# Attention scores by pairs of heads: cross products over 128 rows, high-by-high products over 64 rows each, in the two halves of the array

## The chip, the cores and the metric

The kernel runs on one core of one Trainium2 chip. A core has TensorE (PE; the profile lists its weight loads apart, as PEld), VectorE (DVE), ScalarE (ACT), GpSimd (POOL) and the queues that issue DMAs, SyncE's (SP) among them. The metric is the time of one execution on the device in microseconds, a median over runs. A difference below 0.2% of it, some 3.4 us, is about what a measurement of this kernel can't tell from no change.

## The reference

Two layers of a diffusion backbone with 512 latent tokens and 256 context tokens, width 1024. The change is in the first layer's attention: 16 heads of 64 channels, four key heads, queries in blocks of 128 tokens. A latent block reads all context keys and the latent keys of its own and its neighbouring blocks.

```python
def block(b):
    ...
    s_ctx = jnp.einsum('bqkgd,bnkd->bkgqn', qb, k_c, preferred_element_type=jnp.float32) * scale
    s_loc = jnp.einsum('bqkgd,bnkd->bkgqn', qb, kb, preferred_element_type=jnp.float32) * scale
    s_loc = jnp.where(valid, s_loc, NEG_INF)
    sink_col = jnp.broadcast_to(sink_g, s_ctx.shape[:-1] + (1,))
    p = jax.nn.softmax(jnp.concatenate([s_ctx, s_loc, sink_col], axis=-1), axis=-1).astype(vb.dtype)
    return (jnp.einsum('bkgqn,bnkd->bqkgd', p[..., :L], v_c)
            + jnp.einsum('bkgqn,bnkd->bqkgd', p[..., L:L + band], vb))
...
q_c = rms_norm((h_c @ w_qkv[:, :qd]).reshape(B, L, N_HEADS, HEAD_DIM), q_gain)
...
s_c = jnp.einsum('bqkgd,bnkd->bkgqn', q_c, k_c, preferred_element_type=jnp.float32) * scale
```

After the attention come its output projection, a SwiGLU feed-forward layer, the second layer's retention and another feed-forward layer. None of these is touched.

## The kernel before

Matrix products are made exact enough by splitting each fp32 operand into a high part, rounded to the array's reduced format (fp32r), and a low part, the remainder. A product of two split operands is then the sum of high by high, high by low and low by high; the projections (`mm3`, L147 to L149) spend one matmul on each of the three.

For the scores a head has only 64 channels, and the kernel uses the array's 128 rows for both parts at once. `make_q` leaves a tile for each head: for an even head `qa` has the high part in rows 0 to 63 and the low part in rows 64 to 127, for an odd head `qb` has them the other way round or, where the tiles are filled by DMA (pairs of heads 2 to 6, L605), the same way round as `qa`. `key_parts` leaves two tiles for each key head: `k1` with high over low, `k2` with low over high. A score is the query tile times `k1` plus the query tile times `k2` (L710): the four products high by high, low by low, high by low and low by high in two matmuls of 128 rows, which accumulate in one PSUM bank.

`attend(g, s, b)` works through one block of 128 queries of the four heads that share key head `g`, for stream `s` (0 latent, 1 context). There are 24 such blocks: for each key head four latent ones and two context ones. `Block.score(i)` makes the scores of head `i`. By the keys that a block reads there are three kinds: the first and last latent blocks have 256 latent and 256 context keys in one bank of 512 columns (two parts), the middle ones 256 context and 384 latent keys in two banks, one after the other (two runs), context blocks 256 keys in one bank. After each bank VectorE adds the mask, takes the minimum and writes the scores out of PSUM (L711). After each second head the softmax follows for the two: L717, the exponentials on ScalarE (L101), L721, the scaling (L725 on ScalarE, L727 on VectorE). Then `turn` transposes the probabilities on TensorE (L736) and copies them out (L738), and `output` multiplies them by the values (L750), which writes the two pairs of heads side by side into 64 partitions each.

The score banks come from a pool of three (`pS`, tile S), so that the fourth bank in the order of the program has to wait until L711 has read the first.

The order within an engine is set by a scheduler, ahead of time: in this stage only the dependences are given, and it interleaves the scores, transposes and value products with the projections of the next heads' queries (L147 to L149). What stands in the order waits for what is ahead of it on the same engine.

Of the kernel before, what the change touches and what calls it, by code (L numbers as in the profile page):

```python
# [8 lines left out]
F32 = mybir.dt.float32  # L9
# [3 lines left out]
ALU = mybir.AluOpType  # L13

P = 128
# [29 lines left out]
PRB = 9  # L45
# [4 lines left out]
def dit_kernel(ctx, tc, xT, cT, crow, small, consts, masks, tabs0, tabs1, jtab, adaQ, adaN, adaT, wst, out):  # L50
    nc = tc.nc
    mult, add, sub = ALU.mult, ALU.add, ALU.subtract
# [9 lines left out]
    def T(pool, cols, tag, bufs, dt=F32):  # L62
        return pool.tile([P, cols], dt, tag=tag, bufs=bufs, name=tag)

    def pj(n=512):
        return T(psJ, 512, "pj", 2)[:, :n]
# [24 lines left out]
    def after(ins, others):  # L91
        for o in others:
            tc.add_manual_dep(ins.ins, o.ins.name, order, reason="table set turn")
# [42 lines left out]
    def next_w(pool, own=2, raw=None, behind=(), late=()):  # L136

        raw = raw or w_raw()
        w = w_parts(pool, own)
        after(split(raw, *w, behind), late)  # L140
        return w
# [259 lines left out]
    mask = T(akv, NM * P, "mask", 1, BF16)  # L401
# [118 lines left out]
    ap = At.enter_context(tc.tile_pool(name="ap", bufs=1, reuse_waits="tile"))  # L520
# [3 lines left out]
    kx, kc = {}, {}  # L524
# [32 lines left out]
    q, stats = {}, {}  # L557

    def make_q(j, raw=None):

        if raw is None:
            w = next_w(ap, 0)
            parts_of = lambda k: (w[0][:, k * P:(k + 1) * P], w[1][:, k * P:(k + 1) * P])
        else:

            rows = [[T(ap, 656, "pr", PRB, F32R)[:, :512] for _ in range(2)] for _ in range(2)]
            for i, (hi, lo) in enumerate(rows):
                split(raw[:, i * 512:(i + 1) * 512], hi, lo)  # L570
            parts_of = lambda k: [t[:, k % 4 * P:(k % 4 + 1) * P] for t in rows[k // 4]]
        qs = T(ap, 64, "qs", 4)[:, 0:36].rearrange("p (f n) -> p f n", f=3)
        sqs, o = [], [None, None]

        def part(s, k0, k1):
            if k0 == 0:
                o[s] = pj(NTOK[s])
            for k in range(k0, k1):
                mm3(o[s], parts_of(k), h[s][k], k == 0, k == KT - 1)

        def shape(s):
            n = NTOK[s]
            sq, qn = t_sq(n), t_hn(n)
            nc.scalar.activation(qn, o[s], AF.Identity, scale=qk_gain[:, 0:1])
            nc.scalar.activation(sq, o[s], AF.Square)
            sqs.append(sq)
            if s == 0:
                sw = t_y(s)
                nc.vector.stream_shuffle(sw, qn, swap16)
                nc.vector.tensor_tensor(qn, qn, rope0[:, 0:512], op=mult)  # L590
                nc.vector.tensor_tensor(sw, sw, rope0[:, 512:1024], op=mult)
                nc.vector.tensor_tensor(qn, qn, sw, op=add)
            qa = T(ap, 512, "q", 9, F32R)
            if s == 0:
                qb = T(ap, 512, "q", 9, F32R)
            else:
                qa, qb = qa[:, 0:SC], qa[:, SC:2 * SC]
            q[2 * j, s] = qa
            q[2 * j + 1, s] = qb
            if 1 < j < 7:  # L600
                hi, lo = T(rp, 512, "y0", 1, F32R)[:, :n], T(rp, 512, "hn", 2, F32R)[:, :n]
                split(qn, hi, lo)
                for e, t in enumerate((qa, qb)):
                    for half, src in enumerate((hi, lo)):
                        nc.sync.dma_start(t[64 * half:64 * half + 64, :].bitcast(F32), src[64 * e:64 * e + 64, :].bitcast(F32))  # L605
                return
            nc.scalar.copy(qa[0:64, :], qn[0:64, :])
            nc.scalar.copy(qb[64:128, :], qn[64:128, :])
            nc.vector.tensor_tensor(qa[64:128, :], qn[0:64, :], qa[0:64, :], op=sub)
            nc.vector.tensor_tensor(qb[0:64, :], qn[64:128, :], qb[64:128, :], op=sub)  # L610

        def norms():
            tot = pj(12)
            for s, sq in enumerate(sqs):
                for b in range(NTOK[s] // P):
                    c = 8 * s + 2 * b
                    nc.tensor.matmul(tot[:, c:c + 2], sq[:, b * P:(b + 1) * P], bd[:, 0:P:64], start=True, stop=True)
            y, u, z = qs[:, 0], qs[:, 1], qs[:, 2]
            neg_half_rstd(y, z, tot, HD)
            nc.vector.scalar_tensor_tensor(u, tot, HD * EPS, y, add, mult)  # L620
            ue = u.rearrange("p (b e) -> p e b", e=2)
            for e in range(2):
                hd = 2 * j + e
                nc.vector.tensor_scalar(ue[:, e], ue[:, e], nsink[:, hd:hd + 1], -4.0 / HD, op0=mult, op1=mult)
                stats[hd] = qs

        def first():
            part(0, 0, 5)

        def second():  # L630
            part(0, 5, KT)
            shape(0)
            part(1, 0, 3)

        def third():
            part(1, 3, KT)
            shape(1)

        return [first, second, third, norms]
# [29 lines left out]
    pS = lambda: T(psA2, 512, "S2", 3)  # L669
# [5 lines left out]
    class Block:  # L675
# [9 lines left out]
        def score(self, i):  # L685
            g, s, b, n = self.g, self.s, self.b, len(self.keys) * P
            hd, nl = 4 * g + i, len(self.lk) * P
            if i % 2 == 0:
                self.st = T(ap, 16, "stat", 4)
            st, c = self.st, 2 * (b + 4 * s)  # L690
            qt = q[hd, s][:, b * P:(b + 1) * P]
            pt = T(ap, 656, "pr", PRB)[:, :n + 1]
            top = stats[hd][:, 1, c + hd % 2:c + hd % 2 + 1]
            nc.gpsimd.tensor_copy(pt[:, n:n + 1], top)
            lo, x0 = st[:, i % 2:i % 2 + 1], self.lk[0] * P if nl else 0

            if nl == 384:
                runs = [(nl, SC, 5 * P, [(0, SC, kc)]), (0, nl, 2 * P, [(0, nl, kx)])]
            elif nl == 0:
                runs = [(0, SC, 5 * P, [(0, SC, kc)])]  # L700
            elif b == 0:
                runs = [(0, n, 3 * P, [(0, nl, kx), (nl, SC, kc)])]
            else:
                runs = [(0, n, 0, [(0, SC, kc), (SC, nl, kx)])]
            for c0, w, m0, parts in runs:
                bank = pS()[:, :w]
                for p0, pw, kk in parts:
                    for r in range(2):
                        keys = kk[g][r] if kk is kc else kk[g][r][:, x0:x0 + pw]
                        nc.tensor.matmul(bank[:, p0:p0 + pw], qt, keys, start=r == 0, stop=r == 1)  # L710
                nc.vector.tensor_tensor_reduce(pt[:, c0:c0 + w], bank, mask[:, m0:m0 + w], 1.0, top, add, ALU.min, lo)  # L711
                top = lo
            self.pr.append(pt)
            if i % 2 == 0:
                return
            y = stats[hd][:, 0, c:c + 2]
            nc.vector.scalar_tensor_tensor(st[:, 2:4], st[:, 0:2], -1.0, y, mult, mult)  # L717
            for e in range(2):
                pt = self.pr[i - 1 + e]
                lnexp(pt, pt, AF.Exp, scale=y[:, e:e + 1], bias=st[:, 2 + e:3 + e], accum_out=st[:, 4 + e:5 + e])  # L720
            nc.vector.reciprocal(st[:, 6:8], st[:, 4:6])  # L721
            for e in range(2):
                pt = self.pr[i - 1 + e]
                if e:
                    nc.scalar.activation(pt[:, :n], pt[:, :n], AF.Identity, scale=st[:, 6 + e:7 + e])  # L725
                else:
                    nc.vector.tensor_scalar(pt[:, :n], pt[:, :n], st[:, 6 + e:7 + e], None, op0=mult)  # L727
            if i == 3:
                self.tt = []

        def turn(self, ki):
            if ki >= len(self.keys):
# [33 lines left out]

    def attend(g, s, b):
        blk = Block(g, s, b)
        for i in range(4):
            blk.score(i)  # L770
        for ki in range(len(blk.keys)):
            blk.turn(ki)
        blk.output()
        return blk.copy
# [94 lines left out]
    for d4 in range(0, KT, 4):  # L869
        wpos[0] = wo0 + max(d4, 2)  # L870
        w = [next_w(wo_p) if d > 1 else wo_w[d] for d in range(d4, d4 + 4)]
# [45 lines left out]
    bank = lambda n: T(psF, 512, n, 2)[:, 0:384]  # L917
# [448 lines left out]
    for hd in range(RH):  # L1366
# [24 lines left out]
        Y, X, kc = W4("Y"), W4("X"), W4("X")  # L1391
        kt, qt = [[T(qa, 512, "gate", 4) for _ in range(2)] for _ in range(2)]
# [144 lines left out]
        for i in range(2):  # L1537
            g, v = chunk(bg + i), chunk(bv + i)
# [16 lines left out]
        r, z = mv[:, 8:12], mv[:, 12:16]  # L1555
# [56 lines left out]
        w = []  # L1612
# [190 lines left out]
    for gsz in FFN_GROUPS:  # L1803
        acts = []
        for i in range(gsz):
            if f < 2:
                acts.append(first[f])
            elif f == 2:
                w = [next_w(fp, behind=norm_end) for _ in range(2)]
# [154 lines left out]
```

## Time and profile before

| | us |
|---|---|
| median of 3 runs (lowest to highest) | 1724.65 (1722.21 to 1725.27) |
| the profiled execution, its own time | 1725.47 |
| its span in the profile | 1723.7 |
| attention stage, from the first score to the last | 99 to 304 |

The profiled execution is 0.8 us above the median and 1.8 us longer than its span. In the profile a line names the place in the kernel: L710 is the score product, L711 the reduction behind it, L736 the transposes, L750 the value products. A matmul's row has its operands' form, as 128\*128 128x256: 128 rows and 128 columns of the array, 256 columns streamed; L750 has 128\*64. The duration of a matmul's row contains its way through the array, and rows overlap: what a matmul costs TensorE in a dense run is the distance from its start to the next one's. Both operands are called f32 in the rows, also where they are in the reduced format.

### The profile page before, as it was taken

How to read it: one execution, taken by the hardware profiler on the slowest of the kernel's cores; microseconds unless marked ns; L12 is line 12 of the kernel's file. 1: busy time of each engine (PE TensorE's matmuls, PEld its weight loads, DVE VectorE, ACT ScalarE, POOL GpSimd, SP SyncE). 2: the span in 40 equal slices, each digit the busy share in tenths (PEclk: the TensorE clock that was granted, in tenths of full speed). 3: DMA queues.
4: the chain of work that ended last, by engine and by line, in shares of the span. 5: the costliest groups of instructions: out<-in, count | busy, mean ns of one | idle time of the engine just before them, and what ended most of it. 6: DMA issues, size and time to landing. Idle time of an engine off the chain costs nothing.

```text
span 1723.7 us, 27805 instructions
## 1 busy us (share of the span) xinstructions
PE 1697.5 (98%) x10876; PEld 1514.5 (88%) x10876; DVE 1341.2 (78%) x2418; ACT 867.9 (50%) x1550; POOL 65.7 (4%) x186
## 2 busy tenths in 40 slices
PE   7999999999999999999999999999999999999999
PEld 5788877899999999999988888898898999899988
DVE  6698889788778788787879857757767898877774
ACT  5587779565433334242555534534525564445442
POOL 0000000000000000000000000000000000000000
PEclk9999999999999999999999999999999999999999
DMA  9612221633244534343443624625624323333322
GB/s 351 240 30 58 62 62 56 208 125 125 78 152 122 159 110 147 113 149 118 147 127 84 197 87 122 176 67 132 183 70 121 100 74 117 104 110 111 98 86 86
DMA packets 63378, 209.57 MB, mean 122 GB/s; under 512 B 7312, under 2 KB 8976, under 8 KB 62992
## 3 DMA queue, kind: packets, MB, share of 16 engines
q1 hardware_dynamic: 53168, 171.63, 31.1%
q0 software_dynamic: 9792, 35.66, 8.4%
q8 instruction: 85, 1.39, 0.3%
q10 hardware_dynamic: 288, 0.52, 0.1%
q14 instruction: 45, 0.37, 0.1%
HBM read 201.75 MB, written 2.10 MB: 118 GB/s over the span
## 4 chain that ended last, share of the span: by engine, by line
PE 85%; DVE 6%; DMA 6%; ACT 2%; issue 1%; SPq 0%; DVEq 0%; ACTq 0%
PE Y L897 14%; PE Z L897 7%; PE pj L147 7%; PE pj L149 7%; PE pj L148 7%; PE Z L1296 6%; PE Y L1285 3%; PE X L897 3%; DMA wraw<-in_wst_dram 3%; PE pj L1296 3%; PE pT L736 2%; PE pO L750 2%; PE S L710 2%; PE X L1285 2%; PE X L149 1%; PE X L147 1%
## 5 line engine op out<-in xcount | busy, mean ns | idle before, releaser
L164 ACT CAST whi<-wraw 128x1024 fp32r<-128x1024 f32 x264 | 276.3, 1051 | 337.8 <-PE Z L149 81.3
L165 DVE TENSOR_TENSOR wlo<-wraw,whi 128x1024 fp32r<-128x1024 f32 x264 | 321.5, 1221 | 80.2 <-ACT whi L164 78.5
L897 PE MATMUL Y<-aq,whi 128*128 128x384 f32 x640 | 173.6, 335 | 0.2 <-ACT hn L1053 0.2
L897 PEld LDWEIGHTS Y<-aq,whi 128*128 128x128 f32 x640 | 116.6, 188 | 1.7 <-ACT hn L1053 1.4
L256 DVE SCALAR_TENSOR_TENSOR res<-pj,mod,res 128x512 f32<-128x512 f32 (+1 forms) x112 | 81.1, 728 | 39.6 <-PE pj L149 39.2
L897 PE MATMUL Y<-aq,wlo 128*128 128x384 f32 x320 | 107.0, 334 | 0.0
L273 DVE CUSTOM_DVE_ANT_0 y<-adaw,crow,small_sb 128x1024 bf16<-128x1024 f32 x64 | 81.9, 1280 | 31.7 <-DMA adaw<-in_adaT_dram 31.4
L1296 PE MATMUL Z<-whi,sA 128*128 128x512 f32 x256 | 80.9, 391 | 0.0
L101 ACT ACTIVATE pr<-pr,stat,qs 128x513 f32<-128x513 f32 (+2 forms) x96 | 74.2, 774 | 9.1 <-DVE stat L717 8.8
L147 PE MATMUL pj<-ax,whi 128*128 128x512 f32 x176 | 69.2, 393 | 0.9 <-DVE res L256 0.9
L149 PE MATMUL pj<-ax,whi 128*128 128x512 f32 x176 | 68.7, 390 | 0.0
L148 PE MATMUL pj<-ax,wlo 128*128 128x512 f32 x176 | 68.6, 390 | 0.0
L147 PE MATMUL pj<-act,whi 128*128 128x512 f32 x168 | 65.6, 390 | 0.0
L148 PE MATMUL pj<-act,wlo 128*128 128x512 f32 x168 | 65.6, 390 | 0.0
L149 PE MATMUL pj<-act,whi 128*128 128x512 f32 x168 | 65.5, 391 | 0.0
L897 PEld LDWEIGHTS Y<-aq,wlo 128*128 128x128 f32 x320 | 60.1, 188 | 0.0
L711 DVE CUSTOM_DVE_ANT_0 pr<-S,mask,qs 128x256 f32<-128x256 f32 (+1 forms) x96 | 53.1, 566 | 7.9 <-PE S L710 5.4
L897 PE MATMUL Y<-sA,whi 128*128 128x256 f32 x304 | 58.1, 277 | 0.0
L1296 PEld LDWEIGHTS Z<-whi,sA 128*128 128x128 f32 x256 | 48.0, 188 | 10.4
L897 PE MATMUL Y<-hx,whi 128*128 128x256 f32 x304 | 56.3, 277 | 0.0
L736 PE MATMUL pT<-const_sb,pr 128*128 128x128 f32 x352 | 53.7, 278 | 1.2 <-ACT tt L738 0.9
L1296 PE MATMUL Z<-wlo,sA 128*128 128x512 f32 x128 | 50.4, 394 | 0.5 <-DVE wlo L165 0.5
(580 smaller groups left out, 5051.2 us busy)
## 6 DMA issues: line engine op xcount, KB each, us to landing
wraw<-in_wst_dram SPq DMA_DIRECT2D x224, 512.0 KB, 3.7
adaw<-in_adaT_dram POOLq DMA_DIRECT2D x48, 512.0 KB, 3.8
adan<-in_adaQ_dram SPq DMA_DIRECT2D x16, 512.0 KB, 9.0
wx<-in_wst_dram SPq DMA_DIRECT2D x16, 512.0 KB, 6.4
adan<-in_adaN_dram SPq DMA_DIRECT2D x12, 512.0 KB, 7.7
wx<-in_wst_dram POOLq DMA_DIRECT2D x12, 512.0 KB, 7.4
adaw<-in_adaT_dram SPq DMA_DIRECT2D x8, 512.0 KB, 4.0
wraw<-in_wst_dram POOLq DMA_DIRECT2D x8, 512.0 KB, 5.6
```

The costliest lines, as they stand in the source:

```text
L101: ins = nc.scalar.activation(*args, **kw)
L147: nc.tensor.matmul(o, whi, xhi, start=first, stop=False)
L148: nc.tensor.matmul(o, wlo, xhi, start=False, stop=False)
L149: return nc.tensor.matmul(o, whi, xlo, start=False, stop=last)
L164: after(nc.scalar.copy(hi, t), behind)
L165: return nc.vector.tensor_tensor(lo, t, hi, op=sub)
L256: return nc.vector.scalar_tensor_tensor(res[d], o, mods[l, s][:, part, d:d + 1], res[d], mult, add)
L273: res.append(nc.vector.tensor_tensor_reduce(junk, w, cr[:, s * 1024:(s + 1) * 1024], 1.0, sm_t[:, C_ADAB + l * 48 + j:C_ADAB + l * 48 + j ...
L736: nc.tensor.transpose(tp[:, a * P:(a + 1) * P], self.pr[(0, 2, 1, 3)[a]][:, ki * P:(ki + 1) * P], ident)
L897: nc.tensor.matmul(o, p, r, start=first and k + i == 0, stop=k == 3 and i == 2, skip_group_check=not first)
L1285: ins = nc.tensor.matmul(o[:, e * SC:(e + 1) * SC], p[:, ws], r, start=first and k + e + i == 0, stop=k == 3 and i == 2, skip_group_check= ...
L1296: ins = nc.tensor.matmul(os[t], p, r, start=first and k + i == 0, stop=k == 3 and i == 2, skip_group_check=by_k or not first)
```

## The change

Heads are scored in pairs. For each part of the keys, the low-by-high and high-by-low products of a head are one matmul over 128 rows, against the key tile whose parts lie the other way round (`keys[1 - e]`); the high-by-high product is a matmul over 64 rows: rows 0 to 63 for the even head, rows 64 to 127 for the odd head. The two 64-row products write different banks. They are kept behind the two cross products in TensorE's order. The low-by-low product is no longer made. For that, the query tiles that are filled by DMA get the odd head's parts the other way round.

```diff
                 for e, t in enumerate((qa, qb)):
                     for half, src in enumerate((hi, lo)):
-                        nc.sync.dma_start(t[64 * half:64 * half + 64, :].bitcast(F32), src[64 * e:64 * e + 64, :].bitcast(F32))
+                        r = 64 * (half ^ e)
+                        nc.sync.dma_start(t[r:r + 64, :].bitcast(F32), src[64 * e:64 * e + 64, :].bitcast(F32))
...
-            pt = T(ap, 656, "pr", PRB)[:, :n + 1]
-            top = stats[hd][:, 1, c + hd % 2:c + hd % 2 + 1]
-            nc.gpsimd.tensor_copy(pt[:, n:n + 1], top)
-            lo, x0 = st[:, i % 2:i % 2 + 1], self.lk[0] * P if nl else 0
+            st, c = T(ap, 16, "stat", 4), 2 * (b + 4 * s)
+            qt = [q[hd + e, s][:, b * P:(b + 1) * P] for e in range(2)]
+            top = [stats[hd][:, 1, c + e:c + e + 1] for e in range(2)]
+            for e in range(2):
+                self.pr.append(T(ap, 656, "pr", PRB)[:, :n + 1])
+                nc.gpsimd.tensor_copy(self.pr[i + e][:, n:n + 1], top[e])
+            x0 = self.lk[0] * P if nl else 0
...
             for c0, w, m0, parts in runs:
-                bank = pS()[:, :w]
+                banks = [pS()[:, :w] for _ in range(2)]
                 for p0, pw, kk in parts:
-                    for r in range(2):
-                        keys = kk[g][r] if kk is kc else kk[g][r][:, x0:x0 + pw]
-                        nc.tensor.matmul(bank[:, p0:p0 + pw], qt, keys, start=r == 0, stop=r == 1)
-                nc.vector.tensor_tensor_reduce(pt[:, c0:c0 + w], bank, mask[:, m0:m0 + w], 1.0, top, add, ALU.min, lo)
-                top = lo
-            self.pr.append(pt)
-            if i % 2 == 0:
-                return
+                    keys = [k if kk is kc else k[:, x0:x0 + pw] for k in kk[g]]
+                    for e in range(2):
+                        cross = nc.tensor.matmul(banks[e][:, p0:p0 + pw], qt[e], keys[1 - e], start=True, stop=False)
+                    for e in range(2):
+                        r = slice(64 * e, 64 * e + 64)
+                        after(nc.tensor.matmul(banks[e][:, p0:p0 + pw], qt[e][r], keys[e][r], start=False, stop=True), [cross])
+                for e in range(2):
+                    lo = st[:, e:e + 1]
+                    nc.vector.tensor_tensor_reduce(self.pr[i + e][:, c0:c0 + w], banks[e], mask[:, m0:m0 + w], 1.0,
+                                                   top[e], add, ALU.min, lo)
+                    top[e] = lo
...
-        for i in range(4):
+        for i in (0, 2):
             blk.score(i)
```

In the changed kernel the lines have other numbers: the cross products are L710, the 64-row products L713, the reduction L716 (L711 before), then L720, L724 and L730 (L717, L721 and L727), the transposes L738 (L736), their copies L740 (L738), the value products L752 (L750).

TensorE, the second pair of heads of the first middle block (`kc` are context keys, `k` latent keys, S with its number a bank), before:

```order
L710 MATMUL S_1437<-kc,q 128x256 x2
L617 MATMUL pj<-const_sb,sq 128x2 x4
L710 MATMUL S_1441<-k,q 128x384 x2
L710 MATMUL S_1447<-kc,q 128x256 x2
L710 MATMUL S_1451<-k,q 128x384 x2
```

and after:

```order
L710 MATMUL S_1439<-kc,q 128x256
L618 MATMUL pj<-const_sb,sq 128x2 x4
L710 MATMUL S_1440<-kc,q 128x256
L713 MATMUL S_1439<-kc,q 128x256
L713 MATMUL S_1440<-kc,q 128x256
L710 MATMUL S_1447<-k,q 128x384
L710 MATMUL S_1448<-k,q 128x384
L713 MATMUL S_1447<-k,q 128x384
L713 MATMUL S_1448<-k,q 128x384
```

Where each bank had its two products and was then free to be read, two banks are now open at once, and the 64-row products stand between 128-row ones.

TensorE again, the second pair of heads of the last latent block of key head 0, before:

```order
L710 MATMUL S_1740<-kc,q 128x256 x2
L710 MATMUL S_1740<-k,q 128x256 x2
L710 MATMUL S_1748<-kc,q 128x256 x2
L710 MATMUL S_1748<-k,q 128x256 x2
L148 MATMUL pj<-h,wlo 128x512
```

and after:

```order
L710 MATMUL S_1743<-kc,q 128x256
L713 MATMUL S_1742<-kc,q 128x256
L713 MATMUL S_1743<-kc,q 128x256
L738 MATMUL pT<-const_sb,pr 128x128 x6
L710 MATMUL S_1742<-k,q 128x256
L710 MATMUL S_1743<-k,q 128x256
L713 MATMUL S_1742<-k,q 128x256
L738 MATMUL pT<-const_sb,pr 128x128 x4
L713 MATMUL S_1743<-k,q 128x256
L738 MATMUL pT<-const_sb,pr 128x128 x4
```

The eight products stood together; now transposes and projections stand among them, and one pair of 64-row products is parted by four transposes. In the whole order 72 of the 80 pairs of L713 stand together (58 of 256 columns, 14 of 384) and 8 are parted, which makes 88 places where TensorE goes from other work to 64-row products and back.

VectorE in the same middle block, its second pair of heads, before:

```order
L711 ISA pr,stat<-S_1437,mask,qs 128x256
L711 ISA stat 128x1
L721 RECIPROCAL stat<-stat 128x2
L717 SCALAR_TENSOR_TENSOR stat<-stat,qs 128x2
L711 ISA pr,stat<-S_1441,mask,stat 128x384
L711 ISA stat 128x1
L727 TENSOR_SCALAR pr<-pr,stat 128x512
L711 ISA pr,stat<-S_1447,mask,qs 128x256
```

and after:

```order
L716 ISA pr,stat<-S_1439,mask,qs 128x256
L716 ISA stat 128x1
L730 TENSOR_SCALAR pr<-pr,stat 128x512
L720 SCALAR_TENSOR_TENSOR stat<-stat,qs 128x2
L716 ISA pr,stat<-S_1440,mask,qs 128x256
L716 ISA stat 128x1
L716 ISA pr,stat<-S_1447,mask,stat 128x384
L716 ISA stat 128x1
```

The reductions are the same ones; they now follow run by run, both heads in turn, and not head by head.

More of the change, by code (lines that the diff above doesn't have):

```diff
@@ L687, in score @@
             hd, nl = 4 * g + i, len(self.lk) * P
-            if i % 2 == 0:
-                self.st = T(ap, 16, "stat", 4)
-            st, c = self.st, 2 * (b + 4 * s)
-            qt = q[hd, s][:, b * P:(b + 1) * P]
-            pt = T(ap, 656, "pr", PRB)[:, :n + 1]
-            top = stats[hd][:, 1, c + hd % 2:c + hd % 2 + 1]
-            nc.gpsimd.tensor_copy(pt[:, n:n + 1], top)
-            lo, x0 = st[:, i % 2:i % 2 + 1], self.lk[0] * P if nl else 0
+            st, c = T(ap, 16, "stat", 4), 2 * (b + 4 * s)
[5 more added lines that the diff above has]
+            x0 = self.lk[0] * P if nl else 0
             if nl == 384:
@@ L705, in score @@
             for c0, w, m0, parts in runs:
-                bank = pS()[:, :w]
+                banks = [pS()[:, :w] for _ in range(2)]
                 for p0, pw, kk in parts:
-                    for r in range(2):
-                        keys = kk[g][r] if kk is kc else kk[g][r][:, x0:x0 + pw]
-                        nc.tensor.matmul(bank[:, p0:p0 + pw], qt, keys, start=r == 0, stop=r == 1)
-                nc.vector.tensor_tensor_reduce(pt[:, c0:c0 + w], bank, mask[:, m0:m0 + w], 1.0, top, add, ALU.min, lo)
-                top = lo
-            self.pr.append(pt)
-            if i % 2 == 0:
-                return
+                    keys = [k if kk is kc else k[:, x0:x0 + pw] for k in kk[g]]
[9 more added lines that the diff above has]
+                    top[e] = lo
             y = stats[hd][:, 0, c:c + 2]
@@ L718, in score @@
             for e in range(2):
-                pt = self.pr[i - 1 + e]
+                pt = self.pr[i + e]
                 lnexp(pt, pt, AF.Exp, scale=y[:, e:e + 1], bias=st[:, 2 + e:3 + e], accum_out=st[:, 4 + e:5 + e])
@@ L722, in score @@
             for e in range(2):
-                pt = self.pr[i - 1 + e]
+                pt = self.pr[i + e]
                 if e:
@@ L727, in score @@
                     nc.vector.tensor_scalar(pt[:, :n], pt[:, :n], st[:, 6 + e:7 + e], None, op0=mult)
-            if i == 3:
-                self.tt = []
+            self.tt = []
         def turn(self, ki):
```

## The prediction

> **What bounds the kernel now.** I read the page first, then the busy time and the chain of the attention stage, since nothing else changes. The page's first part and the head of its chain:
>
> ```profile
> PE 1697.5 (98%) x10876; PEld 1514.5 (88%) x10876; DVE 1341.2 (78%) x2418; ACT 867.9 (50%) x1550; POOL 65.7 (4%) x186
> PE 85%; DVE 6%; DMA 6%; ACT 2%; issue 1%; SPq 0%; DVEq 0%; ACTq 0%
> ```
>
> TensorE is busy nearly always, and 85% of the chain that ends last is its work. The attention stage by itself, its busy times and then its chain by line:
>
> ```profile
> core 0: us, PE busy (x) PEld busy (x) DVE busy (x) ACT busy (x) POOL busy (x), PEclk, DMA share, GB/s
> 99.00:304.00 205.00, 197.33 (x1414) 161.28 (x1413) 175.01 (x577) 167.35 (x382) 15.77 (x94) 0.99 0.20 55
> by line: PE S L710 17.6%; PE pT L736 17.5%; PE pO L750 16.4%; PE pj L147 9.9%; PE pj L148 9.4%; PE pj L149 9.4%; DVE pr L711 4.0%; PE pj L617 3.7%; issue 2.4%; ACT pr L101 1.3%; DVE pr L727 1.1%; DVE tt L738 1.0%; ACT tt L738 0.8%; DVE q L6
> ```
>
> In 205 us TensorE is idle for 205.00 - 197.33 = 7.7 us. VectorE (85% busy) and ScalarE (82%) are loaded too, but 84% of the chain lies on TensorE's lines. So a microsecond of TensorE's work added here moves the end by most of a microsecond, while one taken away soon meets VectorE and ScalarE, which have 30 and 38 us of idle time to give. The cost of the change is counted on TensorE.
>
> **What is removed.** The score products, all of them, from the answer on their line:
>
> ```profile
> L710 PEld LDWEIGHTS S<-kc,q x192: 186/188/338, 99.7 to 301.5; 128*128 128x128 f32 x192
> L710 PE MATMUL S<-kc,q x192: 274/282/580, 99.8 to 301.6; 128*128 128x256 f32 x192
> L710 PEld LDWEIGHTS S<-k,q x128: 186/188/247, 99.5 to 301.7; 128*128 128x128 f32 x128
> L710 PE MATMUL S<-k,q x128: 274/336/449, 99.5 to 301.8; 128*128 128x256 f32 x64, 128*128 128x384 f32 x64
> ```
>
> There are 320 matmuls, 256 of 256 columns and 64 of 384, in 80 groups of four: two heads, one part of the keys. Their rows overlap, so what one costs is read from starts in the timeline of TensorE, where scores stand close together (start, duration, engine, line, operation, shapes, count):
>
> ```profile
> 100.05 0.40 PE L710 MATMUL S<-k,q 128*128 128x256 f32 x2
> 100.29 0.40 PE L710 MATMUL S<-kc,q 128*128 128x256 f32 x2
> 100.52 0.40 PE L147 MATMUL pj<-h,whi 128*128 128x512 f32 x1
> 125.31 0.34 PE L710 MATMUL S<-k,q 128*128 128x384 f32 x1
> 125.48 0.39 PE L710 MATMUL S<-kc,q 128*128 128x256 f32 x2
> ```
>
> Two of 256 columns take 0.24 us, one 0.12; one of 384 takes 0.17. A group now has two such matmuls and two of 64 rows. If these run side by side, the second costs nothing, and a group loses one matmul of four. That holds where the two stand next to each other in the order: 58 pairs of 256 columns and 14 of 384, so 58 x 0.12 + 14 x 0.17 = 9.3 us less. The eight parted pairs save nothing.
>
> That two products in different parts of the array can run side by side, the value products show; they write 64 columns of the array each. They show too what it costs to get in and out of that:
>
> ```profile
> 237.43 0.39 PE L147 MATMUL pj<-h,whi 128*128 128x512 f32 x1
> 237.66 0.39 PE L148 MATMUL pj<-h,wlo 128*128 128x512 f32 x1
> 237.89 0.39 PE L149 MATMUL pj<-h,whi 128*128 128x512 f32 x1
> 238.20 1.08 PE L750 MATMUL pO<-tt,v 128*64 128x256 f32 x8
> 239.22 0.50 PE L147 MATMUL pj<-h,whi 128*128 128x512 f32 x1
> 239.56 0.40 PE L148 MATMUL pj<-h,wlo 128*128 128x512 f32 x1
> ...
> 136.94 2.38 PE L750 MATMUL pO<-tt,v 128*64 128x256 f32 x20
> 139.25 0.99 PE L736 MATMUL pT<-const_sb,pr 128*128 128x128 f32 x7
> ```
>
> A run of 20 takes 139.25 - 136.94 = 2.31 us, a run of 8 takes 239.22 - 238.20 = 1.02. Twelve more cost 1.29, or 0.215 for each two. Eight would then take 0.86, so 0.16 us of each run is no streaming.
>
> **What is added: 88 ways in and out.** From the same rows. Ahead of the run, L149 to L750 takes 238.20 - 237.89 = 0.31, where L147 to L148 of the same form takes 0.23: 0.08 on the way in. Inside the run, the 0.16 from above. Behind it, L147 to L148 takes 239.56 - 239.22 = 0.34 for 0.23: 0.11, a weight load that nothing covered. Scores ahead of and behind a run show the same:
>
> ```profile
> 125.71 0.40 PE L710 MATMUL S<-k,q 128*128 128x256 f32 x2
> 126.04 2.38 PE L750 MATMUL pO<-tt,v 128*64 128x256 f32 x20
> 128.35 0.50 PE L710 MATMUL S<-kc,q 128*128 128x256 f32 x2
> 128.69 0.41 PE L710 MATMUL S<-k,q 128*128 128x256 f32 x2
> L750 PEld LDWEIGHTS pO<-tt,v x352: 132/137/138, 117.5 to 313.5; 128*64 128x64 f32 x176
> ```
>
> Two scores and the way in take 0.33 for 0.24 (0.09 more), two scores behind the run 0.34 for 0.24 (0.10 more). One run of value products thus costs 0.08 + 0.16 + 0.11 = 0.35 us beyond its streaming. I read the 0.16 as one exposed weight load of 64 columns and the way out. The load that a 64-row score product needs has 128 columns, and its rows are 188 ns against 137: 0.05 more. So a way in and out costs 0.40 us, if splitting the array by rows behaves as splitting it by columns does. No row of this trace splits it by rows; that is the choice on which the forecast rests, and 0.40 comes from the nearest rows there are. The other end is nothing, if the two halves of the rows need no change of state.
>
> The Trainium skill bears on this choice: "TensorEngine Tiling (Array Packing)", section Key Properties, says that a change of tiling mode, not merely of the tile, drains TensorE, and it lists the forms of 64 rows as a mode of their own. The trace agrees for columns (0.08 in); that it holds for rows no run here shows.
>
> Sum on TensorE: 88 x 0.40 = 35.2 us added, 9.3 taken away, 26 more. Where transposes follow, the uncovered load is shorter, and three runs are followed directly by value products and share a way; I take 2 off: 24.
>
> **What else moves.** Two waits pull in opposite ways. The answer on waits for the weight loads and matmuls of the scores, and the reductions that they wait for, by form:
>
> ```profile
> PEld S L710 <- DVE stat L711: 5.8, 15, 0.7
> PE S L710 <- DVE stat L711: 2.4, 7, 0.5
> L711 DVE CUSTOM_DVE_ANT_0 pr<-S,mask,qs 128x256 f32<-128x256 f32 x64 | 29.8, 478 | 5.5 <-PE S L710 3.7 <-PE pT L736 1.0 <-issue 0.5
> L711 DVE CUSTOM_DVE_ANT_0 pr<-S,mask,qs 128x512 f32<-128x512 f32 x32 | 23.5, 742 | 2.4 <-PE S L710 1.7 <-POOL pr L694 0.5 <-issue 0.2
> ```
>
> TensorE waits 8.2 us for banks now. When its own work gets longer, such waits shrink, up to the 7.7 us of idle time. Against that, two of three banks are open at once: in a middle block the second cross product of the second run needs the bank whose reduction (0.48) can only start after the 64-row products, and TensorE has just one cross product (0.17) to do in the meantime. Some 0.3 us stay uncovered, in 16 such pairs and at about as many passages from one pair to the next: between 0, where the order has transposes or projections in that place (as it has for several), and 32 x 0.3 = 9.6 us. Behind the waiting product all of TensorE's work is queued, projections included. I take 6 of the 7.7 back and add 2: 4 less.
>
> The first reduction of a pair starts two products and a way in later, about 0.4 us in each of 48 pairs. VectorE's 30 idle microseconds hide that; uncovered it would already be in the waits above. The DMAs of L605 are as many and as large, on the same queue at the same places; POOL's 94 copies come two at once on an engine that is busy 16 of 205 us, so both cost nothing. The weight splits and the second half of the kernel are unchanged and start later by what the stage loses.
>
> Forecast: 24 - 4 = 20 us more. The profiled execution's 1725.5 would become 1745.5; it lies 0.8 above the median of the runs shown, which makes 1745.
>
> **The rivals.** *No change of state for rows* ends on the other side. A 64-row load fills its half while the other half works, and the way in and out costs nothing; TensorE loses the 9.3 us. A third of that meets VectorE and ScalarE, so 6 us less: 1719. For it speaks that nothing here splits by rows; against it that 64 columns, also half of the array, cost 0.35, at each of the runs shown. It decides where a way in and out costs less than 9.3 / 88 = 0.106 us; the way in by itself is 0.08.
>
> *Loads covered.* Only the passages cost (0.08 in, and 0.16 - 0.05 = 0.11 out), the loads run ahead. 88 x 0.19 = 16.7, less 9.3 is 7.4, less 2 for waits: 1730. Against it speaks the 0.11 behind each run of value products.
>
> Here too a page has a rule: "TensorE: Matmul & The Clock Gate", Part 3, What overlaps and what doesn't, lets a weight load overlap with matmuls in flight only where the row groups differ. By it the second half's load is covered and the first one's is not, which leaves the forecast as it is.
>
> *Not side by side.* The two 64-row products follow each other, as one would if both used a path in common. Then the 9.3 is not saved either: 1754. Against it speak the value products, of which two take 0.215 together, where a second after the first would have to show in that number.
>
> **How the numbers follow.** The forecast gets 0.65, no change of state 0.12, loads covered 0.13, not side by side 0.10. Faster by over 0.2% (3.4 us) needs most of the first rival's gain: 0.09. Within 0.2%: the rest of it and a little of the second, 0.05. Slower: 0.86. The range reaches from the low edge of the second rival, 1728, to the third with most of the 9.6 us of waits, 1760; it leaves out the first rival and the tails.
>
> **What would show it.** In the changed kernel's timeline, a cross product to the 64-row product behind it should take 0.20 rather than 0.12, the two 64-row products should start within hundredths of each other, and from them to the next cross product 0.3 us or more should pass, with 0.11 more behind that one; each of the 88 places should look alike. If the next product comes 0.12 after the 64-row ones, the first rival holds. The stage from the first score to the last should last about 225 us rather than 205, with VectorE's and ScalarE's busy times unchanged. Two 64-row starts that lie 0.1 or more apart mean the third rival. The forecast is wrong if the stage gets longer by waits for L716 rather than by distances between matmuls.

## The result and the profile after

| | us |
|---|---|
| before, median of 6 runs | 1724.55 |
| changed, median of 6 runs (lowest to highest) | 1754.31 (1752.04 to 1758.88) |
| ratio, with its 95% interval | 1.0179 (1.0165 to 1.0193) |
| the changed kernel's profiled execution, and its span | 1753.82, 1752.1 |

The change costs 29.8 us by the medians (28.4 between the two profiled executions); 20 were forecast. All of it lies in the attention stage. One execution of one experiment's kernel (64-row products in context blocks alone) took 3420 us, and what is said of that kernel below leaves this execution out. The page's first part and the head of the chain, after:

```profile
PE 1728.1 (99%) x10876; PEld 1520.3 (87%) x10876; DVE 1344.6 (77%) x2418; ACT 869.1 (50%) x1550; POOL 65.4 (4%) x186
PE 88%; DVE 5%; DMA 4%; ACT 2%; issue 1%; SPq 0%; DVEq 0%; ACTq 0%
```

TensorE has 30.6 us more of busy time for the same number of matmuls; VectorE and ScalarE have 3.4 and 1.2 more. The stage from the first score to the last, in the windows of the kernel before and of the changed one, under the same header:

```profile
core 0: us, PE busy (x) PEld busy (x) DVE busy (x) ACT busy (x) POOL busy (x), PEclk, DMA share, GB/s
99.50:301.80 202.30, 194.63 (x1393) 158.92 (x1393) 172.33 (x572) 164.79 (x378) 15.77 (x94) 0.99 0.20 54
```
```profile
99.60:331.80 232.20, 225.44 (x1393) 163.24 (x1392) 174.47 (x571) 166.93 (x378) 15.43 (x94) 0.94 0.18 49
```

The stage is 29.9 us longer with the same work on VectorE and ScalarE. One number is new: TensorE's clock, 0.99 before, is 0.94. The new products, from the answer on their line, and a stretch of the changed kernel's timeline on TensorE at full clock:

```profile
L713 PE MATMUL S<-kc,q x96: 379/381/579, 100.8 to 330.4; 64*128 64x256 f32 x96
L713 PE MATMUL S<-k,q x64: 379/436/579, 100.0 to 331.8; 64*128 64x256 f32 x32, 64*128 64x384 f32 x32
```
```profile
195.35 0.39 PE L149 MATMUL pj<-h,whi 128*128 128x512 f32 x1
195.58 0.28 PE L710 MATMUL S<-kc,q 128*128 128x256 f32 x1
195.79 0.39 PE L713 MATMUL S<-kc,q 64*128 64x256 f32 x2
196.11 0.50 PE L710 MATMUL S<-k,q 128*128 128x256 f32 x2
196.54 0.38 PE L713 MATMUL S<-k,q 64*128 64x256 f32 x2
196.85 0.39 PE L710 MATMUL S<-kc,q 128*128 128x256 f32 x1
197.08 0.40 PE L147 MATMUL pj<-h,whi 128*128 128x512 f32 x1
```

From a cross product to the 64-row pair takes 195.79 - 195.58 = 0.21 us where 0.12 is its streaming: 0.09 in. The pair takes 196.11 - 195.79 = 0.32 and 0.31 where 0.12 would be streaming: 0.20 for its own load and the way out. The two crosses behind it take 0.43 from the start of the first to the next pair: 0.24 of streaming, 0.09 of the next way in, and 0.10 for the load that nothing covered. That is 0.39 for one way in and out. Both 64-row products of a pair have their rows merged in one line; in the trace their starts lie 3 to 4 ns apart, and none of the 72 adjacent pairs is an exception.

Rows ahead of the first slow stretch, which starts at 155.4, and then rows inside it, at half clock, from the timeline a little earlier:

```profile
152.77 0.38 PE L710 MATMUL S<-kc,q 128*128 128x256 f32 x1 [0.38 <-DVE stat L716]
153.08 0.38 PE L713 MATMUL S<-kc,q 64*128 64x256 f32 x2
153.39 0.39 PE L710 MATMUL S<-kc,q 128*128 128x256 f32 x1
...
157.40 0.63 PE L148 MATMUL pj<-h,wlo 128*128 128x512 f32 x1
157.83 0.63 PE L149 MATMUL pj<-h,whi 128*128 128x512 f32 x1
158.26 0.41 PE L710 MATMUL S<-k,q 128*128 128x256 f32 x1
158.60 0.58 PE L713 MATMUL S<-k,q 64*128 64x256 f32 x2
159.11 0.58 PE L710 MATMUL S<-kc,q 128*128 128x256 f32 x1
```

A projection of 512 columns takes 0.43 instead of 0.23, a pair with its way out 0.51 instead of 0.31. The windows of these stretches, of the changed kernel and then of the one that the kernel before has in the stage:

```profile
155.40:165.60 10.20, 10.20 (x34) 7.36 (x32) 5.93 (x28) 5.43 (x18) 0.55 (x3) 0.50 0.18 41
244.10:247.50 3.40, 3.40 (x16) 2.85 (x15) 2.65 (x10) 1.29 (x4) 0.00 (x0) 0.50 0.44 100
274.80:288.50 13.70, 10.98 (x37) 7.00 (x36) 10.75 (x38) 10.47 (x28) 0.73 (x4) 0.50 0.15 41
```
```profile
256.60:260.00 3.40, 3.21 (x14) 2.85 (x14) 2.89 (x15) 3.34 (x8) 0.00 (x0) 0.50 0.01 2
```

27.3 us of the stage run at half clock, where it was 3.4.

I summed the stage from the distances between the starts of its matmuls: to each its streaming at full clock by the dense runs, what the change of state adds, what half clock adds, and the rest as waits. The third column is the first experiment below. (The sums run to a few products behind the last score, hence up to 0.8 above the stage. The row for the value products fits the 22 runs of the kernel before at the 0.16 inside a run; their way in and the load behind them stand in the last row, which so holds more than waits. The parting of streaming from the last row is good to some 2 us, as it depends on which distances are taken as dense.)

| us on TensorE | before | pairs, all over 128 rows | changed |
|---|---|---|---|
| stage, first to last score | 202.3 | 207.1 | 232.2 |
| streaming | 173.3 | 174.0 | 166.0 |
| ways into 64 rows and back | 0 | 0 | 33.5 |
| ways of the value products | 3.5 | 3.5 | 3.3 |
| half clock | 1.2 | 2.4 | 8.3 |
| waits and the rest | 24.8 | 27.8 | 21.9 |

### The profile page after: what moved, and what is told of

It reads as the page before. It is cut to its first block, busy times and chain, and to the rows that moved or that the text cites. A ratio compares the mean times of both kernels' runs of the same rounds, so it can differ in the third digit from the quotient of the medians.

```text
span 1752.1 us, 27820 instructions
## 1 busy us (share of the span) xinstructions
PE 1728.1 (99%) x10876; PEld 1520.3 (87%) x10876; DVE 1344.6 (77%) x2418; ACT 869.1 (50%) x1550; POOL 65.4 (4%) x186
## 4 chain that ended last, share of the span: by engine, by line
PE 88%; DVE 5%; DMA 4%; ACT 2%; issue 1%; SPq 0%; DVEq 0%; ACTq 0%
PE Y L899 14%; PE pj L147 7%; PE Z L899 7%; PE pj L148 7%; PE pj L149 7%; PE Z L1298 5%; PE Y L1287 4%; PE X L899 3%; PE pT L738 3%; PE pj L1298 3%; PE pO L752 2%; DMA wraw<-in_wst_dram 2%; PE S L710 2%; PE X L1287 2%; PE S L713 2%; PE X L149 1%
## 5 line engine op out<-in xcount | busy, mean ns | idle before, releaser
L716 DVE CUSTOM_DVE_ANT_0 pr<-S,mask,qs 128x256 f32<-128x256 f32 (+1 forms) x96 | 53.6, 569 | 23.1 <-PE S L713 20.1
L738 PE MATMUL pT<-const_sb,pr 128*128 128x128 f32 x352 | 58.1, 294 | 0.5 <-ACT tt L740 0.3
L738 PEld LDWEIGHTS pT<-const_sb,pr 128*128 128x128 f32 x352 | 41.9, 148 | 13.5 <-issue 6.9
```

Source lines behind the costliest of these rows:

```text
L738: nc.tensor.transpose(tp[:, a * P:(a + 1) * P], self.pr[(0, 2, 1, 3)[a]][:, ki * P:(ki + 1) * P], ident)
```

## The experiments

All start from the changed kernel. Theory A: each of the 88 ways costs 0.39 us, and TensorE then works so thinly that its clock is lowered. The rivals: B, the order by pairs and its score banks; C, the two 64-row products do not run side by side.

**Pairs, all over 128 rows.** The same order by pairs, nothing split by rows.

```diff
-                        after(nc.tensor.matmul(banks[e][:, p0:p0 + pw], qt[e][r], keys[e][r], start=False, stop=True), [cross])
+                        after(nc.tensor.matmul(banks[e][:, p0:p0 + pw], qt[e], keys[e], start=False, stop=True), [cross])
```

> Scores in pairs as in the changed kernel, two banks open at once, but the second product of a head runs over all 128 rows again (high by high and low by low), so nothing is split by rows. Theory A (each of the 88 ways into 64-row products and back costs 0.39 us, and TensorE then works so thinly that its clock is lowered): none of that is left, 1723 to 1730 us, the clock as before (one slow stretch in the attention stage). Rival B (the cost is the order by pairs and its waits for score banks, not the 64 rows): 1745 us or more, with the waits of the score products behind the reduction as long as in the changed kernel.

Measured: 1728.69 us, ratio 1.0025 (1.0015 to 1.0034), mean clock of its runs 0.997. From the answers on the waits of this kernel and of the changed one:

```profile
PEld S L710 <- DVE stat L716: 10.1, 24, 1.0
PE S L710 <- DVE stat L716: 4.2, 11, 0.7
```
```profile
PEld S L710 <- DVE stat L716: 7.8, 19, 0.7
PE S L710 <- DVE stat L716: 3.1, 10, 0.5
```

Rival B is real but small: the order by pairs costs 4.3 us, and the waits for banks are 14.3 us where the kernel before has 8.2. They are even longer than in the changed kernel (10.9), which is 25.6 us slower; so those 25.6 come with the 64-row products and not with the banks.

**One half left out.** The odd head's 64-row product is not made.

```diff
                     for e in range(2):
-                        cross = nc.tensor.matmul(..., start=True, stop=False)
-                    for e in range(2):
-                        r = slice(64 * e, 64 * e + 64)
-                        after(nc.tensor.matmul(banks[e][:, p0:p0 + pw], qt[e][r], keys[e][r], start=False, stop=True), [cross])
+                        cross = nc.tensor.matmul(..., start=True, stop=e == 1)
+                    r = slice(0, 64)
+                    after(nc.tensor.matmul(banks[0][:, p0:p0 + pw], qt[0][r], keys[0][r], start=False, stop=True), [cross])
```

> The odd head's 64-row product is left out (its scores lack high by high); 80 ways in and out instead of 88. Theory A: the two 64-row products run side by side, so the second costs nothing where they stand together; only the 8 ways fewer are saved, 3 us: 1749 to 1754 us. Rival C (they do not run side by side): 72 x 0.13 = 9 us and the 3 less: 1742 us or below.

Measured: 1761.46 us, 1.0211 (1.0194 to 1.0228), mean clock 0.986. Its timeline (the 64-row product is L712):

```profile
194.70 0.38 PE L712 MATMUL S<-k,q 64*128 64x256 f32 x1
195.01 0.38 PE L710 MATMUL S<-kc,q 128*128 128x256 f32 x1
```

One product takes the same 0.31 us from start to start as two in the changed kernel. Rival C falls. The kernel is not faster by the 8 ways fewer, though, but 7 us slower than the changed one, with less work and a lower clock; neither theory expected that. Its four executions differ: the profiled one took 1755.09 us at a clock of 0.989, the other three 1761.4 to 1761.8 at 0.984 to 0.985. In the profiled one the score products wait 19.1 us for banks, where the changed kernel has 10.9; so rival B's cost comes up here too, and how much of it the lowered clock brings on is not shown.

**By head.** Cross product, its 64-row product, next head.

```diff
-                    for e in range(2):
-                        cross = nc.tensor.matmul(...)
-                    for e in range(2):
-                        r = slice(64 * e, 64 * e + 64)
-                        after(nc.tensor.matmul(...), [cross])
+                    halves = []
+                    for e in range(2):
+                        r = slice(64 * e, 64 * e + 64)
+                        cross = nc.tensor.matmul(...)
+                        after(cross, halves)
+                        halves = [nc.tensor.matmul(...)]
```

> The same products, but head by head: cross product, then its 64-row product, then the next head's; 160 ways in and out, none shared, nothing side by side. Theory A: 160 x 0.39 = 62 us on TensorE against the kernel before, nothing saved: 1780 to 1795 us, more if the clock is lowered longer than in the changed kernel. Rival B (order by pairs and banks): a bank is finished earlier, so fewer waits: 1725 to 1745 us. If rows split without a cost, about 1725.

Measured: 1798.46 us, 1.0423 (1.0405 to 1.0441), mean clock 0.979. Its timeline (cross L712, 64 rows L714):

```profile
104.15 0.28 PE L712 MATMUL S<-k,q 128*128 128x256 f32 x1
104.36 0.38 PE L714 MATMUL S<-k,q 64*128 64x256 f32 x1
104.67 0.38 PE L712 MATMUL S<-kc,q 128*128 128x256 f32 x1
104.98 0.38 PE L714 MATMUL S<-kc,q 64*128 64x256 f32 x1
105.29 0.50 PE L149 MATMUL pj<-h,whi 128*128 128x512 f32 x1
```

Each product of 0.12 takes 0.31. The time is 74 us above before: 62 were counted for 160 ways, and the lowered clock is in the rest.

**Filled.** Useless cross products in the places where TensorE waits in context blocks.

```diff
                     for e in range(2):
+                        for _ in range(0 if nl or e else 3):
+                            nc.tensor.matmul(banks[e][:, p0:p0 + pw], qt[e], keys[1 - e], start=True, stop=True)
+                        last = [cross] if e else []
                         cross = nc.tensor.matmul(...)
+                        after(cross, last)
```

> The changed kernel, with the even head's cross product of the context blocks made three times more into the same bank (each overwrites the last), 48 matmuls of 0.12 us = 5.8 us of useless work in 16 places where TensorE waits for a bank; 90 ways in and out. Theory A with the clock (some 10 of the 30 us come from 27 us at half clock, after thin stretches in context blocks): the slow stretches get fewer and the time falls, 1742 to 1750 us, clock 0.995 or above. Rival (the clock costs nothing, TensorE only waits there): the same or up to 6 us more, 1754 to 1760 us.

Measured: 1752.98 us, 1.0164 (1.0149 to 1.0179), mean clock 0.9965. The windows in which the changed kernel had its first two slow stretches:

```profile
155.00:166.00 11.00, 11.00 (x62) 7.99 (x64) 8.60 (x38) 8.12 (x25) 0.68 (x4) 1.00 0.31 85
244.00:248.00 4.00, 4.00 (x35) 3.35 (x36) 2.89 (x5) 2.64 (x4) 1.10 (x4) 1.00 0.00 0
```

The clock recovered there, as theory A has it, but the time lies between the two bands: the useless work seems to have lain on the path for the most part, since the waits of the cross products for banks fell only from 10.9 to 8.7 us. 5.8 us of added work at no added time fits a clock that costs several microseconds; taken alone it shows no more.

**64-row products in context blocks alone, and in latent blocks alone.**

```diff
-  ... qt[e][r], keys[e][r] ...
+  ... qt[e] if nl else qt[e][r], keys[e] if nl else keys[e][r] ...      # context blocks alone
+  ... qt[e][r] if nl else qt[e], keys[e][r] if nl else keys[e] ...      # latent blocks alone
```

> Order by pairs; 64-row products in the 16 groups of the context blocks alone, all others over 128 rows: 16 ways in and out. Against the same order with no 64-row products (1728.7 us): by the ways alone 16 x 0.38 less 16 x 0.1 saved, 4.5 us more, 1731 to 1735 us. If the lowered clock is a cost of its own, brought on by the thin stretches in context blocks, stretches at half clock appear there and some 5 us come on top: 1737 to 1742 us.

> The reverse: 128-row products in the context blocks, 64-row products in the latent ones; 72 ways in and out. By the ways alone, the changed kernel's 1754.3 less 16 x 0.38 plus 16 x 0.1: 1750 us. If the lowered clock costs some 7 us there and comes from the context blocks: clock 0.995 or above and 1743 to 1747 us.

Context blocks alone: 1735.4 us, 1.0060 (1.0046 to 1.0074), mean clock 0.9945; this lies between the two bands and decides nothing. So it ran again:

> The kernel with 64-row products in the context blocks alone once more, for a profile of an ordinary execution (the profiled one ran at about half speed throughout). 1733 to 1738 us; if the lowered clock comes from the context blocks, one to three stretches at half clock in the attention stage where the same order with 128-row products has 6.8 us of it, and each of the 16 ways costs 0.38 us as in the changed kernel.

1734.95 us, 1.0064 (1.0045 to 1.0082), at the upper edge of the first band, that of the ways alone; so the time by itself does not tell the two apart. The stage has one slow stretch, at the beginning of the last key head, which starts with a context block:

```profile
258.50:272.20 13.70, 11.74 (x41) 7.52 (x43) 10.98 (x43) 10.40 (x28) 0.73 (x4) 0.50 0.14 41
```

The pairs over 128 rows have 6.8 us there. Latent blocks alone: 1746.22 us, 1.0126 (1.0110 to 1.0141), mean clock 0.995, in the band of the clock theory and below the 1750 of the ways alone. Its stage has one slow stretch as well, of 13.7 us at the beginning of the last key head: the first two stretches of the changed kernel are gone, but the longest comes up in either half of the change, and not from the 64-row products of the context blocks alone.

**Twice, and grouped.** Each 64-row product made twice; and in banks with two parts, all four cross products ahead of all four 64-row products.

```diff
-                    for e in range(2):
+                    for n2, e in enumerate((0, 1, 0, 1)):        # twice
...
+                for p, (p0, pw, keys) in enumerate(todo):        # grouped: crosses of both parts,
+                    for e in range(2):
+                        cross = nc.tensor.matmul(..., start=p == 0, stop=False, skip_group_check=True)
+                for p, (p0, pw, keys) in enumerate(todo):        # then their 64-row products
```

> Each 64-row product made twice (high by high counts double in the scores): 99 ways in and out, 87 more steps of side-by-side products than in the changed kernel. If only the change of state costs: 11 x 0.38 + 87 x 0.13 = 15.5 us more, 1762 to 1772 us, the lower end where the denser work keeps the clock up. If each 64-row product needs a weight load that nothing covers, another 9 us: 1775 us or more.

> Where a bank has two parts (first and last latent blocks), both parts' cross products come first and then their four 64-row products: the same products, 73 ways in and out instead of 88. If the ways cost 0.38 each: 5.7 us less, 1744 to 1752 us. If the cost is by product and not by way: no change, 1754 us.

Twice: 1771.1 us, 1.0265 (1.0250 to 1.0279), mean clock 0.990; the clock did not stay up with the denser work, against what was expected. Grouped: 1745.76 us, 1.0122 (1.0109 to 1.0136), mean clock 0.995. Their timelines, twice first:

```profile
104.07 0.50 PE L713 MATMUL S<-kc,q 64*128 64x256 f32 x4
104.50 0.39 PE L710 MATMUL S<-kc,q 128*128 128x256 f32 x1
```
```profile
104.21 0.39 PE L715 MATMUL S<-k,q 64*128 64x256 f32 x2
104.43 0.28 PE L715 MATMUL S<-kc,q 64*128 64x256 f32 x2
104.64 0.38 PE L710 MATMUL S<-kc,q 128*128 128x256 f32 x1
```

Four products take 0.43 where two take 0.31: once inside, a further pair costs 0.12, its load covered. The price is for the way, and not for the product.

**The sum over all kernels.** Each run lists its mean granted clock; (1 - clock) times its time is the clock it missed. From the pairs over 128 rows to the changed kernel there are 25.6 us, 88 ways and 10.1 us more of missing clock; to the one with latent blocks alone 17.5 us, 72 ways and 3.3. Two equations give 0.21 us a way, net of what is saved and of waits that shrink, and 0.7 us for a microsecond of missing clock (one microsecond more or less in either difference moves the 0.7 by 0.2). The other kernels were not used for these two numbers. (Added work: twice 87 x 0.13, filled 48 x 0.12, by head the saving that is lost, 160 x 7.3/88.)

| kernel | ways | missing clock | added work | sum | measured |
|---|---|---|---|---|---|
| pairs over 128 rows | 0 | 5.4 | | start | 1728.7 |
| changed | 88 | 15.5 | | used | 1754.3 |
| latent blocks alone | 72 | 8.7 | | used | 1746.2 |
| context blocks alone, second run | 16 | 10.0 | | 1735.3 | 1735.0 |
| grouped | 73 | 8.7 | | 1746.4 | 1745.8 |
| filled | 90 | 6.1 | 5.8 | 1753.9 | 1753.0 |
| one half | 80 | 25.1 | | 1759.3 | 1761.5 |
| twice | 99 | 18.1 | 11.3 | 1769.7 | 1771.1 |
| by head | 160 | 37.8 | 13.3 | 1798.2 | 1798.5 |

Six kernels that the two numbers were not taken from lie within 2.2 us. The sums are rough where the saving does not follow the number of ways: with the full 0.39 for the 15 ways that grouped has fewer and the 11 that twice has more they are 1743.7 and 1771.7, still within 2.2; with 9.3 us of saving in place of the ledger's 7.3, by head comes to 1801.8, 3.3 too high. That one half left out makes the kernel slower is in it too: 19.7 us more of missing clock than the pairs over 128 rows. Among runs of one kernel it goes the same way: context blocks alone took 1732.7 us at a clock of 0.996 and 1737.3 at 0.993, and one half 6.5 us less at 0.989 than at 0.985, with not a line changed.

No version beats the kernel before; the nearest, pairs over 128 rows, is 4.3 us slower.

## Why the prediction was right, and where it was short

**What bounds it: right.** TensorE's time moved the end. The stage grew by 29.9 us, to 232.2, the kernel by 29.8; about 225 had been named for the stage.

**What is removed: right in kind.** The 64-row products run side by side wherever they are adjacent. All 72 counted pairs (58 of 256 columns, 14 of 384) start together, so the 9.3 us were saved; the ledger has 7.3, and the difference is within what its parting of streaming from waits is good for.

**The choice on which the forecast rested: right.** Rows behave as columns did. 0.40 was taken from the value products; it measures 0.39, and the 88 ways 33.5 us, where 35.2 less 2 was forecast. The first rival (no change of state) and the second (loads covered) fall with the same rows: 0.21 in, 0.31 for the pair, 0.10 more behind it. The trace agrees with the rule of the Trainium skill, "TensorEngine Tiling (Array Packing)", Key Properties, that a change of mode drains TensorE: 0.09 us is lost on the way into 64 rows, though no run separates a drain from another cause.

**The third rival hit the measured time and was wrong.** "Not side by side" gave 1754, and 1754.31 was measured. The starts 3 to 4 ns apart and the kernel with one half left out refute it. A time that fits proves no mechanism. The prediction's own argument against this rival was weak: two value products take 0.215 us together, and two products of 256 columns one after the other, at 0.12 each, would take 0.24, hardly more. That the value products run side by side is in their starts, which lie 6 to 7 ns apart in the trace of the kernel before.

**What else moves: this step was mis-sized.** I weighed waits that shrink against waits that are new and took 4 us off. For the order alone, the pairs over 128 rows measured 4.3 us more. With the ways added, waits then shrink by 5.9 on the ledger, so that the changed kernel waits 2.9 less than before; that half was near, as far as the ledger's 2 us allow.

**A term was missing: the clock.** The sum priced every passage at full clock. The stage has 27.3 us at half clock for 3.4, 7.1 us more by the distances between starts. Against the pairs over 128 rows these distances give 8.3 - 2.4 = 5.9, and the sum over all kernels, 0.7 x 10.1 = 7.1. On the ledger of starts the difference is 33.5 for ways, less 7.3 of streaming, plus 7.1 of clock, less 2.9 of waits, less 0.2: 30.2, where the forecast had 33.2, 9.3, 0 and 4. The sign that I named for an error, waits for L716 in place of distances between matmuls, did not come (10.9 us of them, for 8.2).

**The range held in part by luck.** It reached to 1760 for the third rival and for up to 9.6 us of new waits. The first was wrong; what filled the place instead were the clock, which the prediction did not have, and the cost of the order.

What stays open is what exactly lowers the clock; no experiment was made on a threshold. The filled kernel points to thin work on TensorE: 48 useless products cleared two of three stretches and left 10.2 us of the third (one of 3.4 us came up elsewhere). The traces say more. In all of them the clock changes only at steps of 3.41 us. I took the attention stage of the kernel before and of nine kernels from here in windows of that length, and added up in each what its products cost at full clock by the distances of dense runs, two side by side counted once. Of 677 windows 68 are followed by one at half clock. In 66 of these the streaming is under 0.41 of the window; in 604 of the other 609 it is above. Ahead of the changed kernel's three stretches it is 0.40, 0.36 and 0.39, ahead of the one in the kernel before 0.21; in the filled kernel no window around the first two places has less than 0.53. So half clock follows little streaming, whether TensorE's rows are busy or not; that 0.41 is the same in another kernel is not shown.

## What to carry to other kernels

Price a change of the array's shape by what it costs to enter and leave, from any shape change that the profile already has: here 0.39 us, against 0.12 saved by each pair of 256 columns, so by this estimate at least four pairs would have to share one visit (no run had more than two different ones). Where TensorE bounds a stage, count also what the gaps do to its clock: where little is streamed, work that is taken out of a stage may come back as time at half clock. And where a rival's number is met, look at the rows before believing it.

## What the runs showed of the hardware that I had not expected

The clock halves while TensorE's rows are busy. In the windows of the changed kernel ahead of and inside its first slow stretch, TensorE is busy for 4.62 and 5.00 of 5 us:

```profile
150.00:155.00 5.00, 4.62 (x32) 3.61 (x31) 2.56 (x10) 2.70 (x8) 0.00 (x0) 1.00 0.45 105
155.00:160.00 5.00, 5.00 (x17) 3.42 (x17) 3.18 (x19) 4.12 (x15) 0.00 (x0) 0.54 0.15 39
```

The slow stretches of the changed kernel's stage last 3.4, 10.2 and 13.7 us, multiples of 3.4. In the last such window ahead of each of the three, TensorE's rows are busy for 3.03, 3.03 and 3.41 us:

```profile
151.96:155.37 3.41, 3.03 (x18) 1.00 0.50 116
240.71:244.12 3.41, 3.03 (x24) 1.00 0.23 55
271.43:274.84 3.41, 3.41 (x20) 1.00 0.00 0
```

(These three lines are of TensorE alone: length, busy time and matmuls, clock, DMA share, GB/s.) The Trainium skill, "TensorE: Matmul & The Clock Gate", Part 1, gives a window of about 3.4 us and a state at half rate, which agrees; its table of the states ties that state to an idle window, and none of these three windows was idle: the rows were busy, with passages and loads in place of streaming.
